# A hybrid decoder layer on one core: new planner prices, other PSUM banks for the trunk, and a re-ordered recurrence in the jobs

## The chip, the core and the metric

The kernel runs on one NeuronCore of one Trainium2 chip. The metric is the device time of one execution in microseconds, as the median of several runs. Times in this text come from the hardware profile of one execution or from the timed runs.

## What is computed

One decoder layer for two groups of requests that share weights: a prompt of 1024 tokens and eight single-token samples, model width 1024, all in float32.

```
h = x + 0.5 * post1(SwiGLU1(pre1(x)))            # d_ff = 2816
P = pre2(h) @ w_in
  group A: differential attention, 4 heads, 2 maps x 64, v 128, rotary, per-head norm
  group B: RWKV-7 time mixing, 8 heads x 64: a matrix state per head, updated token by token
           s = s * w_t + (s @ -kk_t) (kk_t * a_t)^T + v_t k_t^T ;  y_t = s @ r_t
h = h + post2(concat(A, B) @ w_out)
h = h + 0.5 * post3(SwiGLU2(pre3(h)))
```

pre and post are RMS norms with a gain. The kernel also returns keys, values, the final matrix states and the last projected rows.

## The kernel before

The 1024 prompt columns and 8 sample columns are cut into two halves, and each half goes through the two FFNs: four *phases* of the *trunk* (phase 0 and 1: first FFN of the halves; 2 and 3: second FFN). Weights are split into a high and a low float32r part, and each product is three float32r matmuls (high x high, high x low, low x high). `s_weights` loads and splits them (tiles `wts_raw`, `wts_w`). Phases 1 and 2 are *wide*: one matmul of 512 columns. Phases 0 and 3 use columns of 256, 260 and 264 and, after a few groups, seven products for eight blocks. Each phase ends in a *tail*, the last group's `down` units (eight output tiles by two column chunks), followed by a norm (`s_tail`, tiles `tail_...` or, for phase 2, `last_...`).

Between the FFNs of a half stand the projection (`proj`), the RWKV *jobs* (`job0`, `job1`), attention (`prep`, `attn`, `fin`), and the output projection (`out` for half 0, `outb` for half 1). The trunk of the next phase runs beside them and fills TensorE: phase 1 beside half 0's jobs and attention, phase 2 beside half 1's. The decode work of the samples (`dec`, `decf`, `decb`) lies beside that too.

There are four jobs in each half, each for two heads, and two run interleaved: jobs 0 and 2 are `jb = 0`, jobs 1 and 3 `jb = 1`. A job has a first part (mixing, decay, norms; its PSUM bank is `dec`, with one product in `cb`), and then, in bank `aux0` or `aux1`, the chunked recurrence: the sequence of 512 is cut into 8 chunks of 64; pair products within chunks (banks `aux` and `cb`); a triangular solve by 31 steps on VectorE, to and from which data goes through DRAM (`Md`, `Xd`); matrices `Z` and products `L`, `R` that do not depend on the state; and last a loop over the chunks. In it, the state `Sd` enters one product, `Z` by `Sd`, the state-free products `L` by `R` add to it in the same bank, VectorE makes the next `Sd` from the bank (`scalar_tensor_tensor`), and ScalarE copies two 64x64 blocks of the bank out to `YN`. In the trace a float32 matmul is two instructions and a transpose one; tiles of the jobs are named `mix_X` or `mix_T` (sets of buffers), `job_w` (L) and `bset_Sd` (state).

The order of all instructions is written by a planner in the kernel (`Kern.run`), on the host: streams (generators) put operations into queues, `price` gives each a cost, `after` the time until another engine sees its result, and `run` picks, engine by engine, what to issue next, by the latest time (`late`) that a pass before found for it. `PASSES` such passes are made, and the plan with the least predicted time is issued. `SLACK`, `MODE` (cost of the first float32r matmul behind another kind), `LAND` (time from a DMA's last packet until its data is seen) are such prices. A stream holds a list of PSUM banks (`self.cur.banks`) and takes them in turn; a tile in a bank waits for all that the tile before it in that bank had. The planner's order within each engine is fixed at run time: an engine waits at an instruction that is not ready, even if a later one is. A generator may say `("wait", key)` or `("lock", key)`; it then puts nothing more until the key is signalled by another generator.

The eight banks are `m0` to `m3`, `aux0`, `aux1`, `cb`, `dec`. The trunk has `m0`, `m1`, in phase 0 also `m2`, `m3` (`SIX`), in phase 3 also `aux1`, and within the seven-product groups `m0` to `m3`, `aux0`, `aux1`. `m2`, `m3` serve `proj`, `out`, `outb`, one attention stream has `m2` with `aux0`, the other `m3` with `aux1`.

Of the kernel before, what the change touches and what calls it, by code (L numbers as in the profile page):

```python
# [20 lines left out]
PSUM = bass.MemoryType.PSUM  # L21

P = 128
# [23 lines left out]
C = 64  # L47
NC = HS // C
# [46 lines left out]
SLACK = 0.02  # L95
PASSES = 8
BIAS = {}
# [8 lines left out]
STICK = 0  # L106
MODE = 0.085
HOLD = 0.6
# [63 lines left out]
TV = 0.2  # L172
LAND = 2.0
MPE = 0.0
# [4 lines left out]
class Op:  # L179
    __slots__ = ("eng", "call", "cost", "load", "columns", "dma", "left", "ready", "start", "end", "seen", "then", "st", "ins", "table", "deps", "tile", "port", "late", "key", "before")  # L180

# [36 lines left out]
class Kern:  # L218
# [167 lines left out]
    def price(o, op, a, k, out, ins):  # L386
# [5 lines left out]
        if "dma" in op:  # L392
# [7 lines left out]
            run = min(runs)  # L400
            o.cost = 1.04 if o.eng == "gpsimd" else 1.4 if op == "page_dma" else 0.47
            o.dma = n * out.shape[0] * 4 / run * (9 + 0.041 * run) / 16e3
        elif o.eng == "tensor":
            m = a[1].shape[1]
            if op == "transpose":
                f, o.cost = 2, 0.003 + 2 * n / 2400
            elif a[1].dtype == FR:
                f, o.cost = 1, max(0.004 + n / 2246, 0.107 * m / P)
            elif a[1].dtype == F32:

                f, o.cost = 4, 0.010 + 4 * max(n, m) / 2400
            else:
                f, o.cost = 1, 0.003 + n / 2400
            o.columns, o.load = f * n * a[1].shape[0] / P, m / 1600
            r, c = a[1].start_partition(), out.start_partition()
            o.tile = r, r + a[1].shape[0], c, c + out.shape[0], out.tensor.name
            o.table = f == 1
        elif o.eng == "vector":
            two = (a[1], a[3]) if op == "scalar_tensor_tensor" else ins if op == "tensor_tensor" else [x for x in ins if tuple(x.shape[1:]) != (1,)]
            wide = [x for x in two if x.space != PSUM]  # L420
            fast = op in ("tensor_copy", "tensor_scalar", "memset") and all(x.space != PSUM for x in (out, *ins)) and len(wide) < 2

            o.port = fast or len(wide) > 1
            o.cost = 0.07 + n / (160 if op == "reciprocal" else 480 if op == "tensor_tensor_scan" else 1920 if fast else 960) \
                + (0.05 if op == "scalar_tensor_tensor" else 0.06 * scalars)
        elif o.eng == "scalar":
            o.cost = (0.06 if ins[0].space == PSUM else 0.093) + n / 1195 + 0.093 * scalars + 0.093 * ("accum_out" in k)
        else:
            o.port = True
            o.cost = (0.2 if op == "scalar_tensor_tensor" else 0.156 if op == "tensor_tensor" else 0.06) + n / (470 if op == "tensor_tensor" else 960)  # L430
# [53 lines left out]
    def run(self):  # L484
# [3 lines left out]
        warm, tick, passed = True, 0, 4096.0  # L488
        rings, tile, size, credit, paced = 0.0, None, None, 0.0, 0.0
        lanes = deque([0.0] * 8)  # L490
        while self.streams:
# [37 lines left out]
            if o.eng == "tensor":  # L529
# [6 lines left out]
                if o.table and not round_:  # L536
                    o.cost += MODE * (size == (t[1] - t[0], t[3] - t[2]))
                round_ = o.table
                size = t[1] - t[0], t[3] - t[2]
# [15 lines left out]
            if o.dma:  # L555
                rings = max(rings, s + (1.69 if o.eng == "gpsimd" else 1.17)) + o.dma
                o.seen = rings + LAND
                if o.eng != "gpsimd":
                    lanes.append(o.seen + 0.1)
                    lanes.popleft()  # L560
# [284 lines left out]
    def two(self, half, dt=FR):  # L845

        return [self.T(self.pool, [P, 4160], f"{'XT'[half]}{j}", dt) for j in range(2)]
# [186 lines left out]
    def s_trunk(self):  # L1034
# [3 lines left out]
        for ph in range(4):  # L1038
# [7 lines left out]
            few = ("m0", "m1")  # L1046
            self.cur.banks = few + {0: SIX, 3: ("aux1",)}.get(ph, ())
            yc = []
# [179 lines left out]
            if ph in FAST:  # L1228
                self.cur.banks = few + (("aux1",) if ph else ("m2", "m3"))
            yield from down(len(groups) - 1, True)  # L1230
        self.signal("trunk")
# [455 lines left out]
    def job(self, pool, i, s, jb):  # L1687
# [125 lines left out]
        yield ("lock", "cb")  # L1813
        pa, pv = self.ps2().rearrange("p (n t) -> p n t", t=C), self.ps(bank="cb").rearrange("p (n t) -> p n t", t=C)
        for n in range(NC):
            for h, q in H:
                mm(pa[q, n, :], U[q, n, h, :], self.ident[q, q], start=True, stop=True)
        for n in range(NC):
            for h, q in H:
                o = H[1 - h][1]  # L1820
                mm(pv[q, n, :], L[o, n, 3 * h, :], R[o, n, h, :], start=True, stop=True)
        A.copy(U[:, :, 0, :], pa)
        A.copy(U[:, :, 1, :], pv)
# [92 lines left out]
        for n in range(NC):  # L1916
            pb = self.ps2().rearrange("p (n t) -> p n t", t=C)
            mm(two(pb[:, 0:2]), two(Z[:, n]), two(Sd), start=True, stop=False)
            for h, q in H:
                mm(pb[:, h], two(L[:, n, 2 * h:2 * h + 2]), R[:, n, h, :], start=False, stop=h == 1)  # L1920
            if n < NC - 1:
# [753 lines left out]
```

## Time and profile before

| | |
|---|---|
| median of 3 runs | 2241.69 us (2241.63 to 2242.61) |
| the profiled execution | 2243.7 us, its span 2241.9 us |
| mean granted TensorE clock | 0.994 |
| busy PE, PEld | 2187.3 us, 1960.6 us |
| busy DVE, ACT, POOL | 1559.9 us, 1085.1 us, 1007.8 us |
| DMA | 338.84 MB, mean 151 GB/s |

Busy time is the union of an engine's instructions; PE is the matmul part of TensorE and PEld its weight loads, which overlap with matmuls. All operations are recorded through one helper, so every row has the line L325, and rows are told apart by the names of tiles: `out<-in`, buffer numbers left out. In rows of groups, after the bar: busy us, mean ns of one, then the engine's idle time just before them and what ended it. In rows of the order of time: start in us, duration in us, engine, what, how many. The granted clock is the share of the full TensorE clock that the throttle let through.

### The profile page before, as it was taken

What the parts mean: (1) busy time and instruction counts of PE and PEld (TensorE: products, weight loads), DVE (VectorE), ACT (ScalarE), POOL (GpSimd) and SP (SyncE); (2) the same over time, 40 slices, a digit from 0 to 9 for tenths busy, and PEclk for the clock granted to TensorE, in tenths of its full rate; (3) what the DMA queues carried; (4) which work ended last, traced back from release to release, by engine and by line L of the source; (5) the groups of instructions that cost most, each with busy time, mean ns of one, the idle gap of its engine ahead of it and who ended that gap; (6) DMA issues with size and microseconds to landing.
All of it is one profiled execution on the core that took longest, in us unless ns stands there. A gap on an engine that the chain in (4) does not pass through costs nothing. (4 is left out here: it accounts for less than half of the span.)

```text
span 2241.9 us, 42167 instructions
## 1 busy us (share of the span) xinstructions
PE 2187.3 (98%) x15551; PEld 1960.6 (87%) x15551; DVE 1559.9 (70%) x3608; ACT 1085.1 (48%) x2233; POOL 1007.8 (45%) x834
## 2 busy tenths in 40 slices
PE   8999999999999989999999999999999999999998
PEld 8999998899887778898887777778888989999998
DVE  7868887656667787647775667776765366777776
ACT  6434444644553347344454445435655455444444
POOL 4545555533333673456453332335443355444443
PEclk9999999999999999999999999999999999999999
DMA  7322233445343674755564534476337838342343
GB/s 262 111 95 87 94 113 124 132 149 140 100 116 103 190 213 132 218 156 164 164 205 156 145 115 129 136 221 199 114 103 220 275 115 290 118 151 99 138 147 108
DMA packets 216088, 338.84 MB, mean 151 GB/s; under 512 B 50731, under 2 KB 130379, under 8 KB 215883
## 3 DMA queue, kind: packets, MB, share of 16 engines
q1 hardware_dynamic: 215594, 335.63, 47.9%
q8 instruction: 123, 2.02, 0.4%
q14 instruction: 83, 0.67, 0.1%
q10 hardware_dynamic: 288, 0.52, 0.1%
HBM read 281.06 MB, written 55.03 MB: 150 GB/s over the span
## 5 line engine op out<-in xcount | busy, mean ns | idle before, releaser
L325 POOL TENSOR_TENSOR wts_w<-wts_raw,wts_w 128x1024 fp32r<-128x1024 f32 (+2 forms) x160 | 301.2, 1886 | 356.8 <-ACT wts_w L325 301.1
L325 PE MATMUL trunk_m<-trunk_xl,wts_w 128*128 128x256 f32 (+2 forms) x2574 | 421.7, 316 | 0.4 <-DVE trunk_xl L325 0.4
L325 PE MATMUL trunk_m<-pre_X,wts_w 128*128 128x512 f32 (+3 forms) x2040 | 390.0, 344 | 9.6 <-ACT wts_w L325 6.0
L325 PEld LDWEIGHTS trunk_m<-trunk_xl,wts_w 128*128 128x128 f32 x2574 | 359.3, 188 | 29.4 <-issue 1.6
L325 PE MATMUL trunk_m<-pre_T,wts_w 128*128 128x512 f32 (+3 forms) x1800 | 364.6, 353 | 6.7 <-DVE trunk_xl L325 6.6
L325 PEld LDWEIGHTS trunk_m<-pre_X,wts_w 128*128 128x128 f32 x2040 | 312.8, 190 | 51.7 <-ACT wts_w L325 6.0
L325 ACT CAST wts_w<-wts_raw 128x512 fp32r<-128x512 f32 (+3 forms) x299 | 242.3, 826 | 211.1 <-PE trunk_m L325 123.0
L325 PEld LDWEIGHTS trunk_m<-pre_T,wts_w 128*128 128x128 f32 x1800 | 285.1, 191 | 47.3 <-issue 4.9
L325 PE MATMUL proj_m<-tail_xl,lin_w 128*128 128x256 f32 (+2 forms) x1920 | 320.9, 322 | 0.5 <-DVE init_E L325 0.5
L325 PEld LDWEIGHTS proj_m<-tail_xl,lin_w 128*128 128x128 f32 x1920 | 270.7, 188 | 35.0 <-issue 9.6
L325 DVE TENSOR_TENSOR trunk_xl<-trunk_xl,trunk_m 128x256 f32<-128x256 f32 (+2 forms) x362 | 172.5, 490 | 53.1 <-PE trunk_m L325 52.2
L325 POOL TENSOR_TENSOR lin_w<-lin_raw,lin_w 128x1024 fp32r<-128x1024 f32 x41 | 99.7, 2432 | 221.4 <-ACT lin_w L325 211.4
L325 POOL TENSOR_TENSOR trunk_xl<-trunk_t,trunk_xl 128x260 fp32r<-128x260 f32 (+3 forms) x87 | 93.7, 1078 | 132.9 <-ACT trunk_xl L325 128.9
L325 DVE TENSOR_TENSOR wts_w<-wts_raw,wts_w 128x1024 fp32r<-128x1024 f32 (+3 forms) x109 | 114.1, 1052 | 13.9 <-ACT wts_w L325 13.5
L325 POOL TENSOR_TENSOR wts_w<-wts_lraw,wts_w 128x512 fp32r<-128x512 f32 x57 | 78.5, 1380 | 60.1 <-ACT wts_w L325 57.4
L325 ACT CAST lin_w<-lin_raw 128x1024 fp32r<-128x1024 f32 x52 | 54.5, 1047 | 74.6 <-PE proj_m L325 54.0
L325 PE MATMUL trunk_m<-comb_T,wts_w 128*128 128x260 f32 x660 | 84.7, 283 | 0.0
L325 PEld LDWEIGHTS trunk_m<-comb_T,wts_w 128*128 128x128 f32 x660 | 81.7, 188 | 0.0
L325 ACT CAST wts_w<-wts_lraw 128x512 fp32r<-128x512 f32 x100 | 58.7, 619 | 38.5 <-POOL wts_lraw L325 12.5
L325 PE MATMUL trunk_aux<-trunk_xl,wts_w 128*128 128x256 f32 (+1 forms) x546 | 75.1, 282 | 0.0
L325 ACT CAST trunk_xl<-trunk_t 128x512 fp32r<-128x512 f32 (+3 forms) x94 | 45.4, 484 | 50.4 <-DVE trunk_t L325 49.7
L325 PEld LDWEIGHTS trunk_aux<-trunk_xl,wts_w 128*128 128x128 f32 x546 | 69.5, 189 | 0.0
(614 smaller groups left out, 4088.0 us busy)
## 6 DMA issues: line engine op xcount, KB each, us to landing
wts_raw<-in_ffn_gate_dram SPq DMA_DIRECT2D x87, 512.0 KB
wts_raw<-in_ffn_up_dram SPq DMA_DIRECT2D x56, 512.0 KB
lin_raw<-in_w_in_dram SPq DMA_DIRECT2D x52, 512.0 KB
wts_raw<-in_ffn_down_dram SPq DMA_DIRECT2D x52, 384.0 KB
wts_raw<-in_ffn_down_dram SPq DMA_DIRECT2D x31, 512.0 KB
wts_w<-Ld SPq DMA_DIRECT2D x22, 512.0 KB
wts_lraw<-in_ffn_down_dram SPq DMA_DIRECT2D x18, 512.0 KB
mix_T<-out_dram SPq DMA_DIRECT2D x36, 256.0 KB
```

Of the source, the lines that this page charges most:

```text
L325: o = Op(eng, lambda: fn(*a, **k), st)
```

## The change

Four parts. (1) Prices and planning: ten passes for eight; `MODE` becomes 0.03 plus 0.00043 per column of the operation before; a DMA that writes DRAM is seen 0.6 us after its last packet and one that loads 1.6 us (both 2.0 before); the issue of a DMA costs 1.14 us with runs of 64 bytes or less, 0.44 with 128 partitions, 0.62 otherwise (0.47 before); a ScalarE copy from PSUM to an output of fewer than 128 partitions and more than two dimensions has a fixed part of 0.16 us for 0.06. (2) The trunk's banks: phase 3 begins with `m0` to `m3` and `aux1`; the tails of phases 1 and 2 wait until the output projection's products of the half before are put, and phase 2's tail has `m0` to `m3`. (3) In a job, `U` is turned by eight full 128x128 transposes in two groups of four, each followed by two copies on ScalarE or VectorE, in place of sixteen 64x64 matmuls with the identity and one copy. (4) In the loop over chunks, the state-free products are issued first and the state's product last, and the chunks alternate between two banks: `aux0` and `cb` for `jb = 0`, `aux1` and `dec` for `jb = 1`.

```diff
-PASSES = 8
+PASSES = 10
...
-MODE = 0.085
+MODE = 0.03
...
-LAND = 2.0
+LAND = 1.6
+STORE = 0.6
...
-            o.cost = 1.04 if o.eng == "gpsimd" else 1.4 if op == "page_dma" else 0.47
+            near = out if out.space != bass.MemoryType.DRAM else ins[0]
+            o.loads = near is out
+            o.cost = 1.04 if o.eng == "gpsimd" else 1.4 if op == "page_dma" else 1.14 if run <= 64 else 0.44 if near.shape[0] == P else 0.62
...
-            o.cost = (0.06 if ins[0].space == PSUM else 0.093) + n / 1195 + 0.093 * scalars + 0.093 * ("accum_out" in k)
+            o.cost = (0.093 if ins[0].space != PSUM else 0.16 if len(out.shape) > 2 and out.shape[0] < P else 0.06) + n / 1195 + 0.093 * scalars + 0.093 * ("accum_out" in k)
...
-                    o.cost += MODE * (size == (t[1] - t[0], t[3] - t[2]))
-                round_ = o.table
+                    o.cost += (MODE + 0.00043 * width) * (size == (t[1] - t[0], t[3] - t[2]))
+                round_, width = o.table, o.wide
...
-                o.seen = rings + LAND
+                o.seen = rings + (LAND if o.loads else STORE)
...
-            self.cur.banks = few + {0: SIX, 3: ("aux1",)}.get(ph, ())
+            self.cur.banks = few + {0: SIX, 3: SIX + ("aux1",)}.get(ph, ())
...
             if ph in FAST:
                 self.cur.banks = few + (("aux1",) if ph else ("m2", "m3"))
+            else:
+                yield ("wait", ("outw", ph - 1))
+                self.cur.banks = few + SIX[:2 * (ph == 2)]
             yield from down(len(groups) - 1, True)
...
-        pa, pv = self.ps2().rearrange("p (n t) -> p n t", t=C), self.ps(bank="cb").rearrange("p (n t) -> p n t", t=C)
-        for n in range(NC):
+        pv = self.ps(bank="cb").rearrange("p (n t) -> p n t", t=C)
+        for g in range(2):
+            pa = self.ps2().rearrange("p (n w t) -> p n w t", n=4, w=2)
+            for n in range(4):
+                tr(two(pa[:, n]), two(U[:, 4 * g + n]), self.ident)
             for h, q in H:
-                mm(pa[q, n, :], U[q, n, h, :], self.ident[q, q], start=True, stop=True)
+                self.copy(U[q, 4 * g:4 * g + 4, 0, :], pa[q, :, h])
...
-        A.copy(U[:, :, 0, :], pa)
         A.copy(U[:, :, 1, :], pv)
...
         for n in range(NC):
-            pb = self.ps2().rearrange("p (n t) -> p n t", t=C)
-            mm(two(pb[:, 0:2]), two(Z[:, n]), two(Sd), start=True, stop=False)
+            pb = self.ps(bank=(f"aux{jb}", ("cb", "dec")[jb])[n % 2]).rearrange("p (n t) -> p n t", t=C)
             for h, q in H:
-                mm(pb[:, h], two(L[:, n, 2 * h:2 * h + 2]), R[:, n, h, :], start=False, stop=h == 1)
+                mm(pb[:, h], two(L[:, n, 2 * h:2 * h + 2]), R[:, n, h, :], start=h == 0, stop=False)
+            mm(two(pb[:, 0:2]), two(Z[:, n]), two(Sd), start=False, stop=True)
```

More of the change, by code (lines that the diff above doesn't have):

```diff
@@ L179 @@
 class Op:
-    __slots__ = ("eng", "call", "cost", "load", "columns", "dma", "left", "ready", "start", "end", "seen", "then", "st", "ins", "table", "deps", "tile", "port", "late", "key", "before")
+    __slots__ = ("eng", "call", "cost", "load", "columns", "dma", "loads", "wide", "left", "ready", "start", "end", "seen", "then", "st", "ins", "table", "deps", "tile", "port", "late", "key", "before")
     def __init__(self, eng, call, st):
@@ L416, in price @@
             o.tile = r, r + a[1].shape[0], c, c + out.shape[0], out.tensor.name
-            o.table = f == 1
+            o.table, o.wide = f == 1, n
         elif o.eng == "vector":
@@ L488, in run @@
         warm, tick, passed = True, 0, 4096.0
-        rings, tile, size, credit, paced = 0.0, None, None, 0.0, 0.0
+        rings, tile, size, credit, paced, width = 0.0, None, None, 0.0, 0.0, 0
         lanes = deque([0.0] * 8)
```

## The prediction, made before the result was known

> **What bounds the kernel.** I read the page's first part, then busy time by stage, then what PE waited for, then PE's groups by shape.
>
> ```profile
> span 2241.9 us, 42167 instructions
> ...
> PE 2187.3 (98%) x15551; PEld 1960.6 (87%) x15551; DVE 1559.9 (70%) x3608; ACT 1085.1 (48%) x2233; POOL 1007.8 (45%) x834
> ```
>
> PE is busy for 2187.3 of 2241.9 us; no other engine passes 70%. So a change pays only in two ways: less matmul time, or fewer of the 54.6 us in which PE stands. The stages (PE busy first, granted clock behind POOL):
>
> ```profile
> 350.00:400.00 50.00, 45.06 (x281) 40.41 (x280) 38.36 (x78) 21.86 (x39) 26.29 (x28) 0.93 0.39 131
> 500.00:790.00 290.00, 283.07 (x2365) 239.57 (x2362) 203.35 (x632) 125.28 (x260) 117.58 (x87) 0.99 0.46 132
> 1250.00:1530.00 280.00, 267.92 (x1899) 211.64 (x1898) 202.10 (x580) 125.85 (x256) 104.10 (x65) 0.99 0.52 148
> 1850.00:1890.00 40.00, 37.21 (x296) 36.73 (x295) 23.05 (x48) 23.82 (x41) 16.87 (x23) 0.96 0.81 273
> 1890.00:2200.00 310.00, 310.00 (x2577) 310.00 (x2577) 231.97 (x489) 140.26 (x293) 148.97 (x135) 1.00 0.39 137
> ```
>
> Where the trunk runs alone (1890 to 2200) nothing is left. The jobs lie in the second and third row: PE stands 6.9 + 12.1 = 19.0 us. At 1850 to 1890, the seam of phase 2 and phase 3, it stands 2.8 us and the clock dips. The largest entry among what PE waited for (total us, times, longest):
>
> ```profile
> PE trunk_m L325 <- DVE trunk_xl L325: 8.0, 5, 3.8
> ```
>
> These are accumulator banks not yet emptied by DVE; the edits at the seam aim at them.
>
> **Part 1: chunks in two banks, state-free products first.** There are 8 jobs of 8 chunks. One turn of the loop in the trace, PE's weight loads marking its order:
>
> ```profile
> 571.00 1.39 PEld L325 LDWEIGHTS proj_m<-tail_xl,lin_w 128*128 128x128 f32 x11
> 572.52 0.30 PEld L325 LDWEIGHTS job_aux<-bset_Sd,mix_X 128*128 128x128 f32 x2
> 572.74 0.53 PEld L325 LDWEIGHTS job_aux<-mix_X,job_w 128*128 128x128 f32 x4
> 573.18 1.36 PEld L325 LDWEIGHTS proj_m<-tail_xl,lin_w 128*128 128x128 f32 x11
> 574.49 0.31 PEld L325 LDWEIGHTS job_aux<-bset_Sd,mix_X 128*128 128x128 f32 x2
> ```
>
> and from the same stretch DVE's and ACT's part:
>
> ```profile
> 573.59 0.34 DVE L325 SCALAR_TENSOR_TENSOR bset_Sd<-job_aux,job_ec,init_bones 128x128 f32<-128x128 f32 x1
> ```
>
> ```profile
> 573.97 0.42 ACT L325 COPY mix_X<-job_aux 64x64 f32<-64x64 f32 x2 [0.55 <-DVE bset_Sd L325]
> ```
>
> Z·Sd is issued at 572.52, the two L·R products at 572.74, DVE makes the next state by 573.93, ACT copies the same bank until 574.39, and only then, at 574.49, does the next Z·Sd go: the turn cannot be shorter than 1.97 us, because the single bank must be emptied. Afterwards the next L·R pair writes the other bank and needs neither state nor copies. The chain becomes Z·Sd, DVE, Z·Sd: 573.59 - 572.52 = 1.07, less the 0.44 us of the pair (572.74 to 573.18), plus DVE's 0.34 and the 0.10 seen from ACT's end to PE's start, about 1.1 us. No matmul is added or removed. As proj matmuls fill the turn, the shorter chain is worth only the time PE stands ahead of Z·Sd:
>
> ```profile
> L325 PE MATMUL job_aux<-bset_Sd,mix_X 128*128 128x128 f32 x64 | 13.2, 287 | 1.5 <-ACT mix_X L325 1.1 <-DVE mix_X L325 0.3
> L325 PE MATMUL job_aux<-bset_Sd,mix_T 128*128 128x128 f32 x64 | 13.0, 284 | 1.7 <-ACT mix_T L325 1.4 <-DVE mix_T L325 0.2
> ```
>
> 1.5 + 1.7 = 3.2 us, nearly all of it (1.1 + 1.4) for ACT's copies, that is, for the bank. Shorter waits are not counted there: before 572.52 the loads had ended at 572.39, while the next one, at 574.49, came 0.05 before the end of its forerunners; so some 0.15 us was lost in one turn of two. Half of 64 turns at 0.15 are 4.8 us at most. The gain lies between 0 (the new order merely puts the wait elsewhere) and 3.2 + 4.8 = 8.0; I take 4.0, nearer to the measured row. If the trunk and proj matmuls that fill the turns were gone, 8 x 8 turns at 1.97 - 1.1 us would count instead, 56 us; they are not gone, since trunk work lies beside all jobs.
>
> The second bank is cb for even jobs and dec for odd ones. Both have other users: dec serves the first part of every job, cb its pair products. Chunks 1, 3, 5, 7 thus queue behind whatever holds that bank. Cost taken as 0 (job lateness is covered by trunk work); without that cover it is rival B.
>
> **Part 2: pairs turned by full transposes.** Removed per job: 16 matmuls of 64x64 (32 instructions). Added: 8 transposes of 128x128.
>
> ```profile
> L325 PE MATMUL job_aux<-init_ident,mix_X 64*64 64x64 f32 x128 | 5.4, 220 | 0.0
> ...
> L325 PE MATMUL job_aux<-init_ident,mix_T 64*64 64x64 f32 x128 | 5.0, 219 | 0.0
> ```
>
> What transposes take stands in an existing group, and at one place in the order of time; the new copies' size stands in a row of ACT:
>
> ```profile
> L325 PE MATMUL job_aux<-init_ident,mix_X 128*128 128x128 f32 x48 | 7.4, 276 | 0.0
> ```
>
> ```profile
> 575.11 0.48 PEld L325 LDWEIGHTS job_dec<-init_ident,mix_T 128*128 128x128 f32 x4
> 575.55 1.25 PEld L325 LDWEIGHTS proj_m<-tail_xl,lin_w 128*128 128x128 f32 x10
> ```
>
> ```profile
> L325 ACT COPY mix_X<-job_aux 64x256 f32<-64x256 f32 x19 | 7.0, 366 | 2.3 <-PE job_aux L325 2.1
> ```
>
> Gone are 5.4 + 5.0 = 10.4 us. Sixty-four transposes cost 64 x 0.11 = 7.0 (four of them took PE's queue from 575.11 to 575.55) up to 64 x 7.4/48 = 9.9. Gain 0.5 to 3.4; I take 2.5, nearer to the queue's spacing, since a busy row counts pipeline tails too. One 128x512 copy per job becomes four of 64x256 at 0.366 us on ACT or DVE: 32 x 0.366 = 11.7 us more in total, against 8 copies saved. ACT is idle for half the span and the result is needed only after the 31-step solve, so 0; if that cover failed, about one 0.37 us copy per group, 8 x 2 x 0.37 = 6 us. The second group of transposes waits for the first group's copies, as the job has one bank there; trunk matmuls stand in between.
>
> **Part 3: trunk banks and waits at the seams.**
>
> ```profile
> 1867.56 1.76 DVE L325 RECIPROCAL last_aux<-trunk_acc 128x256 f32<-128x256 f32 x1 [1.27 <-ACT trunk_acc L325]
> ```
>
> ```profile
> 1870.10 7.59 PE L325 MATMUL trunk_m<-pre_T,wts_w 128*128 128x264 f32 x48 [2.77 <-DVE trunk_xl L325]
> ```
>
> ```profile
> 1870.80:1874.20 3.40, 3.40 (x18) 3.40 (x17) 2.33 (x6) 1.89 (x2) 3.40 (x5) 0.50 1.03 381
> ```
>
> DVE is held by a reciprocal; m0 and m1, the tail's only banks, stay full; phase 3's first gate waits 2.77 us; and the granted clock then is 0.50 for 3.4 us (1.7 us lost). With m2 and m3 in phase 2's tail and m2, m3 and aux1 in phase 3 there are two more banks to fill meanwhile. A tail unit is nine matmuls, 42 of which took 5.21 us in the trace:
>
> ```profile
> 1859.84 5.21 PE L325 MATMUL trunk_m<-trunk_xl,wts_w 128*128 128x256 f32 x42
> ```
>
> so a unit is 1.1 us and two more banks are 2.2 us of tail; a gate unit of phase 3 is 24 matmuls, 7.59 / 2 = 3.8 us of cover each. That is more than the wait. Gain 0 to 2.8 + 1.7 = 4.5; I take 4.0. What is late next is the weight conversion on ACT and POOL. The new wait (tail after out's weights) holds only the trunk's tail units, and all of its weights behind them:
>
> ```profile
> L325 PE MATMUL out_m<-out_X,lin_w x384: 275/281/388, 904.9 to 982.3; 128*128 128x256 f32 x192
> ```
>
> ```profile
> L325 PE MATMUL outb_m<-outb_T,lin_w x384: 276/283/474, 1713.3 to 1795.6; 128*128 128x264 f32 x96, 128*128 128x256 f32 x96
> ```
>
> ```profile
> 1084.85 7.34 PE L325 MATMUL trunk_m<-pre_T,wts_w 128*128 128x256 f32 x60
> ```
>
> out ends at 982, and phase 1 turns to its 256-wide units, the tail behind them, only at 1084.85. outb ends at 1796; phase 2's tail, 16 units of nine matmuls at 0.124 us, 18 us in all, is under way at 1859.84, so it begins after 1842 or so. Both waits are met over 40 us early: cost 0. Were out 100 us later, the trunk would stand.
>
> **Part 4: prices.** LAND, STORE, MODE, the DMA and copy prices and PASSES cost nothing on the chip; they re-order 42167 instructions. Where I can look, the rows side with the new ones. The 64x256 copy takes 0.366 (old price 0.27, new 0.37). The way through DRAM:
>
> ```profile
> 656.27 2.56 SPq L325 DMA_DIRECT2D Xd<-job_hres  x4
> ...
> 660.26 1.82 SPq L325 DMA_DIRECT2D bset_TT<-Xd  x4
> ```
>
> The four stores took 2.56 / 4 = 0.64 us each to issue (old price 0.47, new 0.62). The last was issued at about 658.2, and the load that reads them could go at 660.26, 2.0 us later (the planner reckoned 1.17 + 2.0 and the transfer, now 1.17 + 0.6 and the transfer). A truer order shortens in-order waits; a new order can also make some. Bounds: plus or minus 6, a third of the jobs' 19.0 us. I take +1.0, for the shared banks' small waits.
>
> **Sum.** -4.0 - 2.5 - 4.0 + 1.0 = -9.5. The profiled execution took 2243.7 us, 1.8 over its span and 2.0 over the median of 2241.69; the saving goes off the median: 2232.2.
>
> **Rivals.**
> A, the gains do not reach the end: PE's waits move to other places and the sum is part 2's least, -0.5, to part 3's alone, -4.0: 2238 to 2241. For it: the loop's turns are full of other matmuls. Against: the 2.5 us for ACT's copies are waits for a bank that now has a twin.
> B, slower: the shared dec bank. The first part of a job holds dec from its lora products (first at 458.8) to its bonus product (first at 478.8), 20 us; a chunk queued behind it makes the whole chain of that job stand, and PE, which is in order, stands at the misjudged step.
>
> ```profile
> L325 PE MATMUL job_dec<-bset_la,bset_wa x16: 589/591/694, 458.8 to 1356.8; 64*128 64x512 f32 x16
> ...
> L325 PE MATMUL job_dec<-mix_T,init_bones x16: 590/592/667, 478.8 to 1385.8; 128*128 128x512 f32 x16
> ```
>
> Four odd jobs at a wait as long as part 3's, 2.8, and one clock dip, 1.7, are 18.0: 2232.2 + 18.0 = 2250. It decides from about three such stands. Against: the planner sees these bank orders.
> C, more: the new order also removes the wait at the first seam (3.8 us, and 0.93 x 50 us of clock, 3.5 lost): 2232.2 - 7.3 = 2225.
> D, the clock: where transposes stand in for matmuls the gate could close. One dip of 1.7 in each of 8 jobs is 13.6: 2246. Against it, most of the 32 transposes of the rows, begun from 1845.9 to 1867.1, lie in a stretch at full clock:
>
> ```profile
> L325 PE MATMUL rows_cb<-init_ident,outb_T x32: 270/272/273, 1845.9 to 1867.1; 128*128 128x128 f32 x32
> ```
>
> ```profile
> 1840.00:1860.00 20.00, 19.98 (x171) 19.81 (x170) 12.56 (x23) 11.43 (x24) 10.23 (x17) 1.00 0.45 136
> ```
>
> The Trainium skill, "TensorE: Matmul & The Clock Gate", Part 4: PE-mode transpose, says that a transpose does not count as PE busy in the same way and that the full clock is not engaged for it. By that rule the time would be rival D's; the trace, with 1.00 there, does not bear it out among other matmuls.
>
> **How the numbers follow.** Forecast 0.54 (2227 to 2237 by itself), A 0.19, B 0.11, C 0.13, D 0.03. A measurement of this kernel tells 0.2% (4.5 us) from no change. Faster: 0.54 + 0.13 + 0.03 of A = 0.70; same: the rest of A and 0.01 of D, 0.17; slower: B and 0.02 of D, 0.13. The range runs from C's 2222 (part 1 at more than taken) to A and part of D, 2245.
>
> **What would show it.** Right: no wait of trunk_m for DVE near 1867 and clock 1.00 there; job_aux waits for ACT copies near 0; the 64*64 identity groups gone and 64 more 128x128 transposes at 0.11; the two stretches of the jobs with under 15 us idle together. Wrong: job_dec or job_cb waits of 2 us and more, new clock dips, or PE's busy sum grown.

## The result and the profile after

The changed kernel takes 2254.04 us (median of 5, 2249.99 to 2255.04) against 2241.63 us for the kernel before, timed beside it: a ratio of 1.0050, 95% interval 1.0038 to 1.0062. It is 12.4 us slower; 2232.2 had been predicted, with a range up to 2245. The profiled execution took 2254.64 us. In its rows the one line of all operations is L326.

The first part of the page of the changed kernel:

```profile
span 2252.4 us, 41764 instructions
...
PE 2199.1 (98%) x15359; PEld 1962.7 (87%) x15359; DVE 1573.3 (70%) x3623; ACT 1087.4 (48%) x2244; POOL 1006.3 (45%) x832
```

There are 192 matmul instructions fewer (256 small ones gone, 64 transposes new), and yet PE is "busy" 11.8 us longer (2199.1 - 2187.3), while the time in which it stands is nearly the same (53.3 for 54.6 us). Busy time that grows while work shrinks says that the matmuls themselves took longer; what they lose at half clock, and in pauses too short to be listed as waits, counts as busy. The stretches with a granted clock of 0.50 add up to 34.3 us, against 28.4 before; half of the difference, 3 us, is lost to the clock. What makes the other 9 us is taken up under part 2 below, and stays open. Busy time by stage of the changed kernel (PE first, granted clock behind POOL):

```profile
350.00:400.00 50.00, 47.61 (x299) 42.08 (x298) 42.87 (x88) 25.15 (x44) 26.42 (x30) 1.00 0.45 148
500.00:790.00 290.00, 278.90 (x2212) 235.16 (x2207) 197.34 (x618) 124.10 (x260) 109.98 (x82) 0.98 0.44 125
1250.00:1530.00 280.00, 270.24 (x1856) 210.41 (x1856) 194.84 (x568) 122.60 (x256) 99.62 (x62) 0.99 0.51 147
1850.00:1890.00 40.00, 40.00 (x337) 39.82 (x337) 23.26 (x45) 22.49 (x42) 16.24 (x27) 1.00 0.64 207
1890.00:2200.00 310.00, 309.49 (x2569) 309.20 (x2568) 224.69 (x489) 142.40 (x291) 146.55 (x136) 1.00 0.42 148
```

Both seams are better than before: the clock is 1.00 in 350 to 400 (0.93 before), and at 1850 to 1890 PE does not stand at all (2.8 us before). In 500 to 790 PE stands 11.1 us instead of 6.9. The loss is made in the first job stretch and what follows it: the product of the norm behind phase 0 (`tail_aux` from `init_rb`) begins at 427.5 us, 4.9 us earlier than before, the last one behind phase 1 at 1172.9, 10.6 us later than before (1162.3), and the end is 10.5 us later. What PE waited for (us, times, longest), the rows of the jobs and the trunk's banks:

```profile
PE job_aux L326 <- DVE mix_X L326: 6.9, 5, 2.7
...
PE trunk_m L326 <- DVE trunk_xl L326: 3.7, 7, 1.2
PE attn_aux L326 <- DVE mix_w L326: 3.5, 1, 3.5
...
PE job_dec L326 <- DVE bset_Sd L326: 2.3, 2, 1.8
...
PE job_aux L326 <- ACT mix_T L326: 1.2, 3, 0.6
...
PE job_aux L326 <- ACT mix_X L326: 0.2, 1, 0.2
```

The wait that part 3 aimed at fell from 8.0 to 3.7 us, and the waits for ScalarE's copies that part 1 aimed at from 2.6 and 2.1 us to 0.2 and 1.2. The new entry is the first one, 6.9 us for VectorE (2.9 before).

**Where it comes from, at one place.** Two of PE's waits in the first job stretch, the second of them the longest there, and the clock behind it:

```profile
673.07 1.09 PE L326 MATMUL job_aux<-mix_X,bset_TT 64*64 64x128 f32 x16 [1.21 <-DVE mix_X L326]
...
684.56 0.67 PE L326 MATMUL job_aux<-mix_X,job_w 128*128 128x64 f32 x2 [2.71 <-DVE mix_X L326]
```

```profile
684.60:691.40 6.80, 6.80 (x28) 5.53 (x29) 4.01 (x6) 0.41 (x2) 0.97 (x1) 0.50 0.31 96
```

Together they cost 1.21 + 2.71 and half of 6.8 us, 7.3 us. The name at the wait is DVE; so the next question is what DVE did. Its rows in the order of time:

```profile
668.37 0.79 DVE L326 COPY mix_X<-job_aux 64x192 f32<-64x192 f32 x2 [1.10 <-PE job_aux L326]
670.79 0.01 DVE L326 LOAD_MASK_SELECT init_rb<-init_rb  x1 [1.63 <-DMA init_rb<-out_dram]
...
671.73 1.19 DVE L326 COPY mix_X<-job_aux 128x256 f32<-128x256 f32 x3
...
681.93 0.01 DVE L326 LOAD_MASK_SELECT init_rb<-init_rb  x1 [2.50 <-DMA init_rb<-out_dram]
...
684.42 0.21 DVE L326 COPY mix_X<-job_aux 64x64 f32<-64x64 f32 x1
```

DVE stood idle 1.63 and 2.50 us at an instruction of the rotary embedding, which has nothing to do with the jobs, because the data it needs had not come back from DRAM; the job's copies (671.73 and 684.42), for which PE then waits, stood behind it in DVE's order. SyncE's issues for that round trip:

```profile
664.03 0.66 SPq L326 DMA_DIRECT2D out_dram<-init_rb  x1
...
667.49 0.63 SPq L326 DMA_DIRECT2D init_rb<-out_dram  x1
...
675.93 0.65 SPq L326 DMA_DIRECT2D out_dram<-init_rb  x1
678.69 0.62 SPq L326 DMA_DIRECT2D init_rb<-out_dram  x1
```

From the issue of a store to that of the load that reads it: 3.46 and 2.76 us; from the issue of the load to DVE's start: 3.30 and 3.24 us. The new prices reckon about 2.2 us for the first (1.17 + the transfer + `STORE` 0.6) and 3.2 for the second (with `LAND` 1.6); the old ones 3.6 each. The plan is made without slack for these, and an engine that works in a fixed order passes each lateness on to everything queued behind.

This is one place, and this load is not the whole of it: summed over the kernel, DVE waits for it less than before (us, times, longest; before, then after).

```profile
DVE init_rb L325 <- DMA init_rb<-out_dram: 16.1, 4, 8.3
```

```profile
DVE init_rb L326 <- DMA init_rb<-out_dram: 7.0, 4, 2.5
```

### The profile page after: what moved, and what is told of

It is laid out like the page before. It is cut to its first block, busy times and chain, and to the rows that moved or that the text cites. A ratio compares the mean times of both kernels' runs of the same rounds, so it can differ in the third digit from the quotient of the medians.

```text
span 2252.4 us, 41764 instructions
## 1 busy us (share of the span) xinstructions
PE 2199.1 (98%) x15359; PEld 1962.7 (87%) x15359; DVE 1573.3 (70%) x3623; ACT 1087.4 (48%) x2244; POOL 1006.3 (45%) x832
## 4 chain that ended last, share of the span: by engine, by line
PE 78%; DVE 7%; DMA 6%; ACT 3%; issue 3%; POOL 1%; SPq 1%; DVEq 0%; ACTq 0%; POOLq 0%
PE trunk_m L326 45%; PE proj_m L326 11%; PE trunk_aux L326 8%; PE job_aux L326 3%; PE out_m L326 2%; PE outb_m L326 2%; PE attn_m L326 2%; PE attn_aux L326 2%; SPq L326 1%; PE job_cb L326 1%; PE job_dec L326 1%; DVE mix_T L326 1%; DVE job_aux L326 1%; ACT mix_T L326 1%; DMA mix_T<-out_dram 1%
## 5 line engine op out<-in xcount | busy, mean ns | idle before, releaser
L326 POOL TENSOR_TENSOR wts_w<-wts_raw,wts_w 128x512 fp32r<-128x512 f32 (+2 forms) x167 | 314.9, 1889 | 388.7 <-ACT wts_w L326 337.6
L326 PE MATMUL trunk_m<-trunk_xl,wts_w 128*128 128x256 f32 (+2 forms) x2586 | 425.3, 317 | 5.6 <-DVE trunk_xl L326 2.4
L326 PE MATMUL trunk_m<-pre_X,wts_w 128*128 128x512 f32 (+3 forms) x2040 | 393.0, 345 | 8.4 <-ACT wts_w L326 5.9
L326 PEld LDWEIGHTS trunk_m<-trunk_xl,wts_w 128*128 128x128 f32 x2586 | 362.5, 189 | 37.1 <-DVE trunk_xl L326 4.3
L326 PE MATMUL trunk_m<-pre_T,wts_w 128*128 128x512 f32 (+3 forms) x1824 | 366.0, 351 | 0.0
L326 PEld LDWEIGHTS trunk_m<-pre_X,wts_w 128*128 128x128 f32 x2040 | 313.5, 191 | 50.1 <-ACT wts_w L326 5.9
L326 ACT CAST wts_w<-wts_raw 128x512 fp32r<-128x512 f32 (+3 forms) x299 | 242.5, 826 | 205.9 <-PE trunk_m L326 126.9
L326 PE MATMUL proj_m<-tail_xl,lin_w 128*128 128x256 f32 (+2 forms) x1920 | 324.5, 322 | 0.7 <-POOL lin_w L326 0.3
L326 PEld LDWEIGHTS trunk_m<-pre_T,wts_w 128*128 128x128 f32 x1824 | 287.2, 190 | 40.3 <-issue 1.7
L326 PEld LDWEIGHTS proj_m<-tail_xl,lin_w 128*128 128x128 f32 x1920 | 270.8, 188 | 35.6 <-issue 10.4
L326 DVE TENSOR_TENSOR trunk_xl<-trunk_xl,trunk_m 128x256 f32<-128x256 f32 (+2 forms) x362 | 172.3, 488 | 56.7 <-PE trunk_m L326 55.0
L326 POOL TENSOR_TENSOR lin_w<-lin_raw,lin_w 128x1024 fp32r<-128x1024 f32 x43 | 103.5, 2408 | 196.8 <-ACT lin_w L326 168.1
L326 POOL TENSOR_TENSOR trunk_xl<-trunk_t,trunk_xl 128x260 fp32r<-128x260 f32 (+3 forms) x86 | 91.3, 1062 | 118.2 <-ACT trunk_xl L326 118.1
L326 DVE TENSOR_TENSOR wts_w<-wts_raw,wts_w 128x1024 fp32r<-128x1024 f32 (+3 forms) x102 | 106.6, 1049 | 18.1 <-ACT wts_w L326 18.0
L326 ACT CAST lin_w<-lin_raw 128x1024 fp32r<-128x1024 f32 x52 | 54.5, 1048 | 87.7 <-PE proj_m L326 63.6
L326 POOL TENSOR_TENSOR wts_w<-wts_lraw,wts_w 128x512 fp32r<-128x512 f32 x52 | 70.2, 1352 | 55.0 <-ACT wts_w L326 53.9
L326 PE MATMUL trunk_m<-comb_T,wts_w 128*128 128x260 f32 x660 | 84.6, 283 | 0.0
L326 PEld LDWEIGHTS trunk_m<-comb_T,wts_w 128*128 128x128 f32 x660 | 81.7, 188 | 0.0
L326 ACT CAST wts_w<-wts_lraw 128x512 fp32r<-128x512 f32 x100 | 58.7, 619 | 41.7 <-PE trunk_m L326 12.1
L326 ACT CAST trunk_xl<-trunk_t 128x512 fp32r<-128x512 f32 (+3 forms) x94 | 45.4, 483 | 58.5 <-DVE trunk_t L326 58.3
L326 PE MATMUL trunk_aux<-trunk_xl,wts_w 128*128 128x256 f32 (+1 forms) x534 | 73.3, 282 | 0.0
L326 ACT CAST wts_w<-wts_dec 128x512 fp32r<-128x512 f32 x32 | 18.8, 587 | 102.6 <-DVE wts_dec L326 92.0
```

Source lines behind the costliest of these rows:

```text
L326: o = Op(eng, lambda: fn(*a, **k), st)
```

## The experiments

Three theories were set against each other at first: (1) the shared banks of the chunk loop, the prediction's rival B; (2) the new order of some 42,000 instructions, by scatter or, in its narrow form, by the new prices; (3) the transposes, rival D. From the fifth run on, P is the landing prices, S the scatter, M the mode and copy prices. Each kernel was timed beside the kernel before; ratios carry 95% intervals.

**One part undone.** Each of the four parts is taken back to the code before, the other three stay. The loop:

```diff
-            pb = self.ps(bank=(f"aux{jb}", ("cb", "dec")[jb])[n % 2])...
+            pb = self.ps2()...
+            mm(two(pb[:, 0:2]), two(Z[:, n]), two(Sd), start=True, stop=False)
             for h, q in H:
...
-            mm(two(pb[:, 0:2]), two(Z[:, n]), two(Sd), start=False, stop=True)
```

> All of the change but the chunk loop, which keeps the order and the single bank of the kernel before. Theory 1 (the shared banks of the chunk loop cost the 12 us: jobs queue behind one another on cb and dec): the loss goes, and what the seams and transposes gained stays, so about 2241.6 - 4.0 - 2.5 = 2235, and the first job stretch goes back to under 155 us. Theory 2 (the new order of 42000 instructions, whatever caused it, scatters the jobs' small waits by about 6 us either way): anywhere from 2236 to 2254, with nothing in common with the other three. Theory 3 (the full transposes cost it): no change, about 2254.

Measured: 2249.75 us, ratio 1.0038 (1.0018 to 1.0057). About a third of the loss goes; rival B wanted all of it to go.

The turning of the pairs, by 64x64 products with the identity:

```diff
-                tr(two(pa[:, n]), two(U[:, 4 * g + n]), self.ident)
...
+                mm(pa[q, n, :], U[q, n, h, :], self.ident[q, q], start=True, stop=True)
```

> All of the change but the full transposes: pairs are turned by sixteen 64x64 products per job as before. Theory 1 (shared banks): 2254 plus the 2.5 us of matmul time that the transposes saved, about 2256. Theory 2 (a new order scatters the waits): 2242 to 2260. Theory 3 (transposes and their four copies per job make the waits and the clock dips): back below 2244.

Measured: 2261.27 us, 1.0106 (1.0073 to 1.0139). The transposes are not the loss.

All prices and the number of passes:

```diff
-PASSES = 10
+PASSES = 8
-MODE = 0.03
+MODE = 0.085
-LAND = 1.6
-STORE = 0.6
+LAND = 2.0
...
```

> All of the change but the planner's new prices and passes. Theory 1 (shared banks): within 4 us of 2254. Theory 2 in its narrow form (the new prices order the job stretches badly): back to about 2240, the waits of job_aux for mix_X under 3 us. Theory 3 (transposes): about 2254.

Measured: 2244.57 us, 1.0020 (1.0005 to 1.0034). Three quarters of the loss go, the most of the four, and `job_aux` waits 0.5 us for `mix_X`, under the 3 us that the narrow form of theory 2 named.

The trunk's banks:

```diff
-            self.cur.banks = few + {0: SIX, 3: SIX + ("aux1",)}.get(ph, ())
+            self.cur.banks = few + {0: SIX, 3: ("aux1",)}.get(ph, ())
...
-            else:
-                yield ("wait", ("outw", ph - 1))
-                self.cur.banks = few + SIX[:2 * (ph == 2)]
```

> All of the change but the trunk's additional banks and the wait of its tail for out's weights. The trace gives the three seams about 12 us of gain between them, so by theories 1 and 3 the time rises by what the seams lose, to about 2258 to 2266, with the wait of trunk_m for DVE of some 2.8 us back at the seam of phases 2 and 3. Theory 2 (scatter): the job stretches change as well, by 6 us either way, though no line of the jobs is altered.

Measured: 2248.99 us, 1.0036 (1.0021 to 1.0051): faster by 5 us, where theories 1 and 3 expected it slower by 4 to 12. Its seams stayed good with the old banks:

```profile
350.00:400.00 50.00, 47.29 (x296) 41.70 (x295) 42.72 (x89) 25.29 (x45) 27.09 (x30) 1.00 0.46 149
...
1850.00:1890.00 40.00, 39.73 (x331) 39.20 (x330) 21.81 (x45) 24.11 (x43) 17.59 (x30) 1.00 0.71 239
```

So what the seams gained here came with the order, not with the banks.

**The prices by themselves, and the size of the scatter.** The fifth run puts back the landing prices only:

```diff
-LAND = 1.6
-STORE = 0.6
+LAND = 2.0
+STORE = 2.0
```

> The whole change, but the planner's landing prices are the old ones for loads and stores alike (2.0 instead of 1.6 and 0.6); MODE, the DMA issue and copy prices and the ten passes stay new. Theory P (the short landing prices make loads follow their stores too closely; SP stands for the store, DVE for the load, and the job's copies behind it on DVE hold PE): DVE's waits of init_rb for its load at 671 and 682 (1.63 and 2.50 us after the change) go, SP's waits for the out_dram stores of init_rb fall from 18.7 to about 6 us, the time comes back to 2242 to 2247. Theory S (any new order scatters the time by some 6 us): 2242 to 2260, and SP's waits have nothing to do with it. Theory M (the mode and copy prices make it): stays at 2250 to 2256.

Measured: 2236.83 us, 0.9987 (0.9972 to 1.0003), 17 us under the whole change. The new `MODE`, issue and copy prices are still in it. DVE's waits at 671 and 682 are gone (0.53 us is left at 676.83); another wait for this load, of 8.1 us, stands at 1353, where PE waits for ScalarE (1.88 us) and not for DVE. The sixth is the kernel before with the price hunk of the diff and nothing else:

> The kernel before with nothing but the new prices and passes. Theory P: slower by about what they cost in the whole change, 9 us, so 2246 to 2252, and SP's waits for the out_dram stores of init_rb rise from 6.2 us to 12 and more. Theory S: 2235 to 2250, either side of before. Rival B of the prediction (shared banks): no change, 2238 to 2244.

Measured: 2257.24 us, 1.0076 (1.0055 to 1.0097). With no bank, product or transpose changed, the prices cost 16.4 us, no less than the whole change does. SyncE's waits for the stores of the rotary embedding (us, times, longest), in the kernel before, in the changed one, in this one, and with the old landing prices:

```profile
SPq L325 <- DMA out_dram<-init_rb: 6.2, 4, 2.8
```

```profile
SPq L326 <- DMA out_dram<-init_rb: 18.7, 11, 3.8
```

```profile
SPq L326 <- DMA out_dram<-init_rb: 17.5, 10, 3.8
```

```profile
SPq L326 <- DMA out_dram<-init_rb: 6.7, 4, 3.1
```

The seventh and the eighth kernel change no price that describes the chip, only the window in which the planner takes two operations as equally early; the seventh in the kernel before, the eighth in the changed one:

```diff
-SLACK = 0.02
+SLACK = 0.021
```

> The kernel before with only the planner's tie window changed, 0.021 instead of 0.020 us: no price, bank or product differs, only the order that comes out. It sizes the scatter. Theory P: a few us either way, 2238 to 2247, and SP's waits for the stores of init_rb stay near 6 us, since the landing prices are the old ones. Theory S: differs from before by 6 us or more.

> The changed kernel with only the planner's tie window changed, 0.021 instead of 0.020 us. Theory P: stays clearly slower than before, 2248 to 2258, with SP's waits for the stores of init_rb above 12 us. Theory S: anywhere from 2240 to 2260, so that the loss of the change may vanish by the mere re-roll.

Measured: 2243.20 us, 1.0011 (0.9998 to 1.0023), and 2251.74 us, 1.0044 (1.0028 to 1.0059). Both moved by little over 2 us, and the loss stayed; SyncE's waits for the stores are 7.3 and 15.5 us, as theory P had it. Two rows of the seventh are worth a look, since it has the trunk's old banks:

```profile
1872.62 0.60 PE L325 MATMUL rows_cb<-init_ident,outb_T 128*128 128x128 f32 x4
1873.48 6.47 PE L325 MATMUL trunk_m<-pre_T,wts_w 128*128 128x264 f32 x48 [0.26 <-ACT wts_w L325]
```

Phase 3 begins here after 0.26 us of waiting instead of 2.77: a mere re-roll removed the wait on which the prediction had built part 3.

**Which landing price.** The ninth run has `LAND = 1.6` and `STORE = 2.0`, the tenth `LAND = 2.0` and `STORE = 0.6`, the eleventh 2.6 for both.

> The whole change, with the store's landing price alone put back (2.0 instead of 0.6); loads keep the new 1.6. Theory P1 (the store price is the one that hurts: stores of init_rb landed 1.7 to 4.6 us after their issue in the changed kernel, the new price reckons 2.2, the old one 3.6): 2234 to 2243, SP's waits for the stores of init_rb at or under 8 us. Theory P2 (the load price hurts: 3.3 us seen from the issue of init_rb's load to DVE's start, 3.2 reckoned): stays at 2248 to 2256.

> The whole change, with the load's landing price alone put back (2.0 instead of 1.6); stores keep the new 0.6. Theory P1 (store price): stays at 2247 to 2256, SP's waits for the stores of init_rb above 12 us. Theory P2 (load price): back to 2234 to 2243.

> The whole change with landing prices of 2.6 for loads and stores, more than the old 2.0. Theory P1: the waits of SP for stores fall a little further, to some 4 us, with little left to gain: 2232 to 2240. Rival: a price longer than the transfer puts loads and what needs them later than they need be, and the time rises again: 2241 to 2250.

Measured: 2252.54 us, 1.0054 (1.0036 to 1.0071); 2245.38 us, 1.0022 (1.0010 to 1.0034); 2245.46 us, 1.0023 (1.0009 to 1.0036). The ninth run speaks against theory P1, the store price alone: SyncE's waits went down, to 9.2 us (8 or less had been expected), and the time did not. The tenth lies between the two theories. The eleventh has hardly any such waits left (1.0 us in 2) and is slower than the fifth all the same. The sum of these waits is a mark of the store price, not a measure of the loss.

**Parts 1 to 3 where the landing prices do no harm.** All four have `LAND = STORE = 2.0`. The twelfth run has besides the old loop (the first run's edit); the thirteenth the old turning (the second's); the fourteenth the old trunk banks (the fourth's). The fifteenth is the twelfth, and the sixteenth the fifth, with `SLACK = 0.021`.

> The change with the old landing prices (the fifth run) and, besides, the old chunk loop: one bank, state product first. It sizes part 1 where the landing prices do no harm. The prediction's -4.0 for the loop: 2241 against the fifth run's 2237. Rival A (the gain does not reach the end): 2235 to 2239. Rival B (the shared banks cost more than they bring): under 2234.

> The change with the old landing prices and the old turning by 64x64 products. The prediction's -2.5 for the transposes: 2239 against the fifth run's 2237. If the transposes are worth more, as 2261 against 2254 under the new landing prices had it: 2243 to 2245. If scatter rules: 2231 to 2237.

> The change with the old landing prices and the old trunk banks and no wait of the tail for out. The prediction's -4.0 for the seams: 2241 against 2237, with trunk_m's wait for DVE of some 2.8 us back near 1867. The traces' own sum for the three seams, 8 us and more: 2245 or above. If the banks bring nothing, as 2249 without against 2254 with them under the new landing prices had it: 2232 to 2237.

> The twelfth run (old landing prices, old chunk loop) with the tie window 0.021 instead of 0.020 us. If the loop costs what the twelfth run said: 2229 to 2235, still under before. If that was a lucky order: 2236 to 2243.

> The fifth run (whole change, old landing prices) with the tie window 0.021 instead of 0.020 us. If prices rule: 2234 to 2241, well under the 2251.7 of the same re-roll with the new landing prices. If the fifth run was a lucky order: 2244 or more.

Measured: 2231.13 us, 0.9959 (0.9945 to 0.9973); 2235.12, 0.9982 (0.9964 to 1.0001); 2241.52, 1.0001 (0.9989 to 1.0014); 2246.36, 1.0033 (1.0019 to 1.0047); 2239.33, 0.9999 (0.9985 to 1.0013). The twelfth is the fastest of all, faster than both kernels; but the fifteenth, the same kernel with another tie window, is 15.2 us slower. That the loop costs something, as the twelfth seemed to say, was a lucky order. The pages of the two, the twelfth first, and what PE waited for longest in the fifteenth:

```profile
PE 2191.0 (98%) x15359; PEld 1959.1 (88%) x15359; DVE 1532.2 (69%) x3595; ACT 1091.5 (49%) x2257; POOL 1019.6 (46%) x847
```

```profile
PE 2196.8 (98%) x15359; PEld 1960.7 (87%) x15359; DVE 1567.0 (70%) x3600; ACT 1084.6 (48%) x2248; POOL 1027.2 (46%) x849
```

```profile
PE job_aux L326 <- DVE mix_T L326: 7.3, 3, 3.4
```

**A second order for each single price.** The seventeenth and the eighteenth run are the ninth and the tenth with `SLACK = 0.021`.

> The ninth run (store price old, load price new) with the tie window 0.021. If the load price of 1.6 does the harm: 2248 to 2257 again. If the ninth run was an unlucky order and the store price does it: 2236 to 2244.

> The tenth run (load price old, store price new) with the tie window 0.021. If the load price does the harm: 2234 to 2244. If the store price does it: 2248 to 2256. If both do a share: 2243 to 2249 as the tenth run.

Measured: 2238.80 us, 0.9992 (0.9980 to 1.0004), and 2249.37 us, 1.0049 (1.0030 to 1.0069). Both re-rolls came out where the store price was to do the harm, against the ninth run. Put together by landing prices, with all kernels that share them:

| `LAND`, `STORE` | kernels | mean us | lowest, highest |
|---|---|---|---|
| 2.0, 2.0 | 9 (before; runs 3, 5, 7, 12 to 16) | 2239.9 | 2231.1, 2246.4 |
| 2.0, 0.6 | 2 (runs 10, 18) | 2247.4 | 2245.4, 2249.4 |
| 1.6, 2.0 | 2 (runs 9, 17) | 2245.7 | 2238.8, 2252.5 |
| 1.6, 0.6 | 6 (after; runs 1, 2, 4, 6, 8) | 2253.8 | 2249.0, 2261.3 |

In the two large groups kernels scatter by a standard deviation of 4.8 and 4.7 us, whatever part they have or lack; the groups do not overlap, and they are 14.0 us apart (with a standard error of 2.5, from these deviations and counts). Five pairs of runs differ in nothing but the two landing prices. For each, how much more there is with the new ones (us; the time is the median of the timed runs, the rest is from the profiled executions, the waits summed over all their rows):

| new, old prices | time | PE stands | at half clock | DVE waits for DMAs | PE waits for DVE |
|---|---|---|---|---|---|
| after, run 5 | 17.2 | 11.0 | 19.9 | 5.9 | 8.3 |
| runs 8, 16 (both re-rolled) | 12.4 | 6.4 | 13.7 | 10.0 | 1.5 |
| runs 1, 12 (old loop) | 18.6 | 22.0 | 9.9 | 7.2 | 18.0 |
| runs 2, 13 (old turning) | 26.2 | 14.9 | 0.7 | 21.7 | 10.1 |
| runs 4, 14 (old trunk banks) | 7.5 | 4.7 | -0.1 | 4.3 | 5.5 |
| mean | 16.4 | 11.8 | 8.8 | 9.8 | 8.7 |

The pair of landing prices is the cause of the loss; that is shown. Its form is seen too: PE stands 11.8 us longer and loses half of 8.8 us to the clock, together 16.2 of the 16.4 us. That VectorE waits longer for DMAs, and PE for VectorE, in every pair agrees with the path seen at 671 and 682; it does not show that all of the loss goes that way (in the sixth run, which has all new prices, VectorE's waits for DMAs are shorter than in the kernel before, 29.8 us for 40.7). How the loss divides between the two prices is not shown: by the means of two, each costs about half, but two orders at a scatter of some 5 us do not tell 6 from 0.

## Why the prediction was wrong

**Part 4, the prices, taken at +1.0: the step that failed.** It measured +16.4 us by itself (2257.24 against 2240.81), and the landing prices alone some 14 by groups and 16.4 by pairs. The prediction saw that a new order can make waits, and bounded that at plus or minus 6, a third of the jobs' idle time. The bound was too narrow: idle time that there is does not limit what a plan can add, and PE's standing time alone grew by 4.7 to 22.0 us in the five pairs, with half clock on top. And it said "the rows side with the new ones" from one round trip, `Xd`, whose store was readable 2.0 us after its issue. The trace of before held a row against it, in the same queue:

```profile
685.18 0.65 SPq L325 DMA_DIRECT2D out_dram<-init_rb  x1
686.01 1.71 SPq L325 DMA_DIRECT2D job_lraw<-Md  x4
688.08 0.63 SPq L325 DMA_DIRECT2D init_rb<-out_dram  x1
```

SyncE stood for this store, as one of the four waits that the list gave, and the load went 2.90 us after it; the new price reckons 2.2. In the changed kernel the trace tells of seven DMAs that began right when such a store landed: 1.76 to 4.61 us after its issue, the median 2.75. A price of 2.2 is over only one of the seven, so the planner puts the reader where it is late more often than not, and such a lateness can stop a whole queue, as at 671 and 682. A price that is too long cost less (2245.46 us in the eleventh run); whether it costs anything is not shown, since this lies within the scatter of the kernels with 2.0.

The Trainium skill, "DMA: Bandwidth & Descriptors", Anatomy of one DMA (written for GpSimd's path; these stores go from SyncE), gives some 2.0 us of fixed cost to a DMA, most of it until the write is confirmed, and calls the delay surprisingly long where the target is HBM; its section Latency and other measured facts says that HBM's own access is 0.2 us on average and 2 us at high load. The smallest value here (1.8) lies near the first, and the 4.6 goes beyond it; that a loaded HBM explains the spread was not tried.

**Part 1, the loop, -4.0: the turn is shorter as foreseen, the loop as a whole is not, and the worth is not shown.** The order is as foreseen. PE's weight loads in the changed kernel:

```profile
573.09 0.53 PEld L326 LDWEIGHTS job_cb<-mix_X,job_w 128*128 128x128 f32 x4
573.54 0.30 PEld L326 LDWEIGHTS job_cb<-bset_Sd,mix_X 128*128 128x128 f32 x2
573.76 0.53 PEld L326 LDWEIGHTS job_aux<-mix_X,job_w 128*128 128x128 f32 x4
574.21 0.30 PEld L326 LDWEIGHTS proj_m<-tail_xl,lin_w 128*128 128x128 f32 x2
574.48 0.30 PEld L326 LDWEIGHTS job_aux<-bset_Sd,mix_X 128*128 128x128 f32 x2
```

From one state product to the next 0.94 us (573.54 to 574.48; 1.97 before, 1.1 foreseen). That is the shortest turn, against 1.78 before (so the 1.97 that the prediction called the least was not); the median of all is 1.65 us, against 2.30 before. But the second bank is not always free when the loop comes to it, which the prediction had taken at a cost of 0 and rival B had feared. One job's first two state products, and the last product between them for which another job's first part had that bank:

```profile
609.29 0.30 PEld L326 LDWEIGHTS job_aux<-bset_Sd,mix_X 128*128 128x128 f32 x2
...
641.52 0.42 PEld L326 LDWEIGHTS job_dec<-mix_T,init_bones 128*128 128x128 f32 x2
...
644.35 0.30 PEld L326 LDWEIGHTS job_dec<-bset_Sd,mix_X 128*128 128x128 f32 x2
```

This turn took 35 us. From the first to the last state product the eight jobs take 183.6 us together, 137.7 before. PE had other work meanwhile, and in the time there is nothing to see: with the loop 2236.8 and 2239.3 us, without it 2231.1 and 2246.4. The waits for ScalarE went, and at other places waits for VectorE came.

**Part 2, the transposes, -2.5: less than foreseen on PE, too small to see in the time.** The groups of the changed kernel:

```profile
L326 PE MATMUL job_aux<-init_ident,mix_T 128*128 128x128 f32 x144 | 22.6, 279 | 3.3 <-DVE job_aux L326 2.3 <-ACT mix_T L326 0.6 <-DVE mix_T L326 0.2
L326 PE MATMUL job_aux<-init_ident,mix_X 128*128 128x128 f32 x80 | 12.6, 278 | 0.6 <-DVE mix_X L326 0.6
```

The 64*64 groups are gone, and 32 + 32 transposes are added (112 and 48 before). By busy sums this is 10.2 us for 10.4, by the spacing from each start on PE to the next 7.7 for 8.8: a gain of 0.2 to 1.1, where 0.5 to 3.4 had been the bounds. Nor did the matmul time as a whole shrink. The third run differs from the kernel before in parts 1 to 3 only; its PE is busy for 2192.1 us, 17.1 of them at half clock (2187.3 and 28.4 before), so that without what the clock took PE is busy some 10 us longer. Which of the three parts makes it so was not tried. The runs say 7 us for the transposes once (2261.3 against 2254.0) and -1.7 the other time (2235.1 against 2236.8), both within the scatter.

**Part 3, the trunk's banks, -4.0: right in the trace, the worth not shown.** The foreseen signs came (8.0 to 3.7 us, clock 1.00 at the seam). Yet the fourth and the seventh run have the old banks and no such wait, while the fourteenth, 4.7 us slower than the fifth, has it again:

```profile
1871.81 7.61 PE L326 MATMUL trunk_m<-pre_T,wts_w 128*128 128x264 f32 x48 [1.90 <-DVE trunk_xl L326]
```

Of the five kernels with the old banks two have such a wait of 1 us or more at phase 3's first gate, of the fifteen with the new ones none, so the banks may well help against it; but the wait belongs to the order as much as to the banks. The runs without the banks are 4.7 us slower once (2241.5 against 2236.8) and 5.1 faster the other time (2249.0 against 2254.0).

**The rivals.** B had the sign, a time near (2250) and the wrong cause: jobs did queue for a shared bank, but the sixth run loses as much with no bank shared. D, the clock by transposes, is out: the fifth run has all the new transposes and is at half clock for 14.3 us, half as long as the kernel before, and the sixth has none of them, and this is its second job stretch (clock 0.96, against 0.99 in the changed kernel):

```profile
1250.00:1530.00 280.00, 268.17 (x1930) 211.27 (x1931) 198.98 (x577) 119.39 (x243) 98.68 (x61) 0.96 0.50 143
```

In the changed kernel each of the seven dips before the last products begins within 2 us of the end of a wait of PE of 1.1 us or more, though not every such wait has one (2.06 us until 753.05 has none). The prediction's rule for being wrong, waits of `job_dec` or `job_cb` of 2 us, new dips, PE's busy sum grown, fired on all counts (2.3 us in two for `job_dec`, the clock at 684.6, +11.8 us), but its first item pointed at banks, and the largest wait was in `job_aux`.

Parts 1 to 3 together, by two orders each with the old landing prices: 2238.1 with them, 2242.0 without (before and seventh run), 3.9 us of the 10.5 foreseen. At this scatter that is not certain, and the other new prices are in it: the third run, with parts 1 to 3 and all the old prices, took 2244.6.

## What to carry to other kernels

Where a planner fixes the order of every queue, its prices are part of the kernel: here a price near the least time that a transfer was seen to take cost some 14 us, and one longer than most cost less, since a late transfer holds a whole queue and what waits behind it on others. Collect all rows of a kind before agreeing to a price, above all those where a queue stood for it. And before an edit is credited with a few us, re-roll the order with a constant that means nothing; here that alone moved one kernel by 15 us and removed a wait that looked structural.

## What the runs showed of the hardware

A VectorE instruction of 128x1 elements took thirteen times its time while GpSimd was at work. In the changed kernel, VectorE and then GpSimd:

```profile
821.40 2.76 DVE L326 SCALAR_TENSOR_TENSOR attn_sm<-attn_sm,aset_nlam 128x1 f32<-128x1 f32 x1
824.20 0.35 DVE L326 SCALAR_TENSOR_TENSOR mix_w<-mix_w,attn_sm 128x128 f32<-128x128 f32 x1
824.46 0.68 DVE L326 TENSOR_REDUCE dec_dreg<-dec_dreg 128x8 f32<-128x512 f32 x1
825.06 0.21 DVE L326 SCALAR_TENSOR_TENSOR attn_sm<-attn_sm,aset_nlam 128x1 f32<-128x1 f32 x1
```

```profile
819.87 1.83 POOL L326 TENSOR_TENSOR wts_w<-wts_raw,wts_w 128x768 fp32r<-128x768 f32 x1
821.67 2.47 POOL L326 TENSOR_TENSOR dec_dreg<-dec_dreg 128x512 f32<-128x512 f32 x2
```

It took 2.76 us where the same operation takes 0.21, and ended at 824.16, within 0.02 us of the end of GpSimd's products (824.14); GpSimd's instruction at 819.87 was under way when it began; most of PE's 3.5 us of `attn_aux` waiting for `mix_w` is this. The Trainium skill, "SBUF — State Buffer", SBUF: two separate sides, says that the two engines hold a common port pair as an exclusive lock for a whole instruction; the row agrees with it as to the blocking, but the instruction came behind more than one of GpSimd's: two that began after it went first. No run took GpSimd's products away there.
